# Shared k and q tiles behind the crossing of a two-way scan, and half matrices stored for its solve

## The chip, the cores and the metric

The kernel runs on one core of a Trainium2 chip. The metric is the device time of one execution in microseconds (us), the median of three runs. A core has five engines that run their own instruction streams beside each other: TensorE (PE in the profile: matmuls and transposes; its weight loads are PEld), VectorE (DVE), ScalarE (ACT), GpSimd (POOL) and SyncE (SP). SyncE issues all DMA transfers of this kernel, in order; 16 DMA engines carry them out.

## The reference

One layer of an encoder over 2048 positions of width 1024. A normalised input goes through one projection, whose columns feed two groups of heads. One group is windowed attention. The other, with four heads of 128, is a gated delta rule that is scanned forwards and backwards, with the outputs summed. Cut to the delta rule of one direction:

```python
decay = jnp.exp(jnp.where(incl, g[..., :, None] - g[..., None, :], -jnp.inf))
m = jnp.where(strict, jnp.einsum('bhncd,bhnsd->bhncs', k_beta, k) * decay, 0.0)
t_inv = triangular_solve(eye + m, eye)           # lower, unit diagonal
u = t_inv @ (v * beta)
w = t_inv @ (k_beta * exp(g))
a_intra = jnp.where(incl, jnp.einsum('bhncd,bhnsd->bhncs', q, k) * decay, 0.0)

def step(state, inp):
    v_new = u_i - w_i @ state
    o = (q_i * exp(g_i)) @ state + a_i @ v_new
    state = state * exp(g_last) + k_dec.T @ v_new
    return state, o

fwd = gated_delta_rule_chunked(q, k, v, g[:, :, 0], beta[:, :, 0])
bwd = flip(gated_delta_rule_chunked(flip(q), flip(k), flip(v), flip(g[:, :, 1]), flip(beta[:, :, 1])))
return fwd + bwd
```

The joined outputs of both groups go through an output projection and are added to the input.

## The kernel before

**Stages.** Phase A projects the input, convolves q, k and v, computes the attention and writes its results to DRAM. For each delta head h, `kq_d[h]` holds k and q there, 128 features by 2 by 2048 positions. Phase B does the delta heads one after the other. The 2048 positions are 16 chunks of 128, taken in four groups of four (c4).

- `pre_front(h)` loads k, q and v by groups, forms the products of k with k and with q for each chunk, and multiplies them by the decays into `ma` (L711). For each group and each direction d, a tile view `ma[d, c4]` holds, for 128 rows and four chunks, slot 0 (the matrix to be inverted) and slot 1 (the intra-chunk matrix). Slot 0 is stored to the DRAM buffer `m_d` at L716, one transfer for a group and direction: 128 rows by 4 chunks by 128 columns of float32.
- `solve(h)` reads only the four 32 by 32 diagonal blocks of each of these matrices back from `m_d`, as X (L739) and L (L740), in runs of 32 elements; inverts all of them at once on VectorE, a column after the other (L749, L753); and stores the inverses to `x_d` (L754).
- `invert(h)` loads these inverses as `xc` (L765), builds the full inverses from them with matmuls (L781), and writes them into slot 0 of `ma`.
- `scan(h)` runs 16 steps i. In each of them direction 0 takes chunk i and direction 1 chunk 15 - i. From step 1 on a step loads its chunk of k and q as `kqc` (L819), 128 KB, into one of four buffers of its direction, multiplies k by the state (`pk`, L821) and q by the state (`po`, L832), and updates the state (L839, L842). The two directions cross between steps 7 and 8: at step 8 direction 0 takes chunk 8, which direction 1 has taken at step 7.
- After step 12, and after the last, `post` normalises the finished groups of outputs. Between these, as work that fills TensorE, output products of the attention half run (`sw_units`, L596 to L598, with loads `mxs`, `xrs`, `zcs` and stores `part`). At the end `out_pair` does the output products of the delta half.

Front, solve and inversion of head h + 1 and the scan of head h overlap: two heads' `ma` tiles are held at a time, in two sets that alternate.

**Order.** The source order isn't the order on the engines. `set_order` builds a graph of all instructions with an estimated cost for each, plans the whole kernel in alternating passes from the front and from the back, keeps the best plan of the later passes, and pins the resulting order of each engine, SyncE's transfers included. A DMA counts there with 500 ns on SyncE, and with a share of a common bus that grows with its runs and their length.

**Lines touched.** L716 (the store of `m_d`), and in `scan` the load at L819 with its tile at L818 and its readers L821 and L832.

Of the kernel before, what the change touches and what calls it, by code (L numbers as in the profile page):

```python
# [7 lines left out]
F32 = mybir.dt.float32  # L8
# [7 lines left out]
P = 128  # L16
# [6 lines left out]
NQ = 8  # L23
EPS = 1e-6
NDEC = 1
LATE = ((0, 2), (1, 2), (1, 3), (0, 3), (2, 2), (3, 2), (3, 3), (2, 3), (4, 2), (5, 2), (6, 2), (7, 2), (7, 3), (6, 3), (5, 3), (4, 3))
WSB = 7
MXB = 8
# [518 lines left out]
def phase_b(ctx, wide, xe, ae, late, tc, t, ident, consts, hp, mix_dn, mix_sw, kq_d, v_d, zdn_d, zsw_d, dp, out):  # L547
    nc = tc.nc
    V, A, G, T = nc.vector, nc.scalar, nc.gpsimd, nc.tensor
    dma = nc.sync.dma_start  # L550
# [71 lines left out]
    halves = slice(0, 64), slice(64, P)  # L622
# [18 lines left out]
    def pre_front(h):  # L641
# [9 lines left out]
        ma = H["ma"] = {}  # L651
        m_d = dp.tile([2, NCH, 4 * (32 * P + 32)], F32, tag="m_d", name=f"m_d{h}", bufs=2)
        x_d = dp.tile([2, NCH, P, 32], F32, tag="x_d", name=f"x_d{h}", bufs=2)
        for n, c4 in enumerate(FRONT):
            s4 = slice(4 * c4, 4 * c4 + 4)
            cs = slice(c4 * 512, (c4 + 1) * 512)
            kq = q2[:, 2 * (n % 2) : 2 * (n % 2) + 2]
            dma(kq, kq_d[h][:, :, cs])
            vt = q2[:, 4 + n % 2]
            dma(vt, v_d[h][:, cs])  # L660
            gms = []
            for d in range(2):
                k = 2 * (n % 2) + d
                if k < 3:
                    gm = q3[:, k].rearrange("p (c i) -> p c i", c=4)
                else:
                    gm = q1.tile([P, 4, P], F32, tag="gm", name=f"dc{h}_{c4}_{d}", bufs=1)
                if h < NDEC:
                    dma(gm.rearrange("p c i -> p (c i)"), dec_d[h, d][c4])
                else:  # L670
                    src = gr_d[d].rearrange("(c h) i -> c h i", h=4)[s4, h]
                    dma(gm, src.partition_broadcast(P))
                    G.tensor_tensor(gm, gm, dmask[:, d : d + 1].to_broadcast([P, 4, P]), ALU.add)
                gms.append(gm)
                p = 3 - c4 if d else c4
                if p not in mp:
                    mp[p] = ma_tile(h, p)
                ma[d, c4] = mp[p][:, :, 1 - d :: 2]
            for j, ss in ((0, ssk), (1, ssq)):
                tr = ps_t.tile([P, 4, P], F32, tag="tr", name=f"tr{h}_{c4}_{j}")  # L680
                for c in range(4):
                    T.transpose(tr[:, c], kq[:, j, c * P : (c + 1) * P], ident)
                if j == 0:
                    ks[c4] = kv_tile("ks", h, n, f"ks{h}_{c4}")
                    A.activation(ks[c4], tr, AF.Copy)
                for c in range(4):
                    cc = 4 * c4 + c
                    src = ks[c4] if j == 0 else tr
                    jk = q1.tile([P, P], F32, tag="jk", name=f"jk{h}_{c4}_{j}_{c}", bufs=3)
                    A.activation(jk, src[:, c], AF.Square, accum_out=ss[:, cc : cc + 1])  # L690
            V.tensor_scalar(ssk[:, s4], ssk[:, s4], EPS, None, ALU.add)  # L691
            G.tensor_tensor(nk[:, s4], ssk[:, s4], pw[:, 0, :4], ALU.pow)  # L692
            V.reciprocal(ssk[:, s4], ssk[:, s4])
            V.tensor_tensor(
                bp[:, :, s4], beta[:, s4, h :: 4].rearrange("p c d -> p d c"),
                ssk[:, s4].unsqueeze(1).to_broadcast([P, 2, 4]), ALU.mult,
            )
            for c2 in range(2):
                gh = ps_g.tile([P, 2, 2, P], F32, tag="gh", name=f"gh{h}_{c4}_{c2}")
                for k in range(2):  # L700
                    c = 2 * c2 + k
                    T.matmul(
                        gh[:, k], kq[:, 0, c * P : (c + 1) * P], kq[:, :, c * P : (c + 1) * P], start=True, stop=True
                    )
                for k in range(2):
                    c = 2 * c2 + k
                    cc = 4 * c4 + c
                    for d in range(2):
                        if h >= NDEC:
                            A.activation(gms[d][:, c], gms[d][:, c], AF.Exp, bias=ngc[:, d, cc, h : h + 1])  # L710
                        V.scalar_tensor_tensor(  # L711
                            ma[d, c4][:, c], gh[:, k], bp[:, d, cc : cc + 1],
                            gms[d][:, c : c + 1].to_broadcast([P, 2, P]), ALU.mult, ALU.mult,
                        )
            for d in range(2):
                dma(m_d[d, s4, : P * P].rearrange("u (i j) -> i u j", j=P), ma[d, c4][:, :, 0])  # L716
            tr = ps_t.tile([P, 4, P], F32, tag="tr", name=f"trv{h}_{c4}")
            for c in range(4):
                T.transpose(tr[:, c], vt[:, c * P : (c + 1) * P], ident)
            vs[c4] = kv_tile("vs", h, n, f"vs{h}_{c4}")  # L720
            for c in range(4):
                cc = 4 * c4 + c
                A.activation(vs[c4][:, c], tr[:, c], AF.Copy, scale=nk[:, cc : cc + 1])
            if h:
                for k in range(FILLF[h - 1][n]):
                    fill(1, bank(k % 2))
# [80 lines left out]
    def scan(h, H):  # L807
        ks, vs, ck, ma = (H[k] for k in ("ks", "vs", "ck", "ma"))
        oacc = H["oacc"] = {}
        st = {}  # L810
        for i in range(NCH):
            for d in range(2):
                c = i if d == 0 else NCH - 1 - i
                c4, cl = c // 4, c % 4
                sc = slice(c * P, (c + 1) * P)
                nm = f"{h}_{d}_{i}"
                if i:
                    kqc = rp.tile([P, 2, P], F32, tag=f"kqc{d}", name=f"kqc{nm}", bufs=4)  # L818
                    dma(kqc, kq_d[h][:, :, sc])  # L819
                    pk = ps_s.tile([P, P], F32, tag="pk", name=f"pk{nm}")  # L820
                    T.matmul(pk, kqc[:, 0], st[d], start=True, stop=True)  # L821
                    r = rp.tile([P, P], F32, tag="r", name=f"r{nm}")
                    V.scalar_tensor_tensor(
                        r, pk, negc[:, d, c, h : h + 1], vs[c4][:, cl], ALU.mult, ALU.add
                    )
                else:
                    r = vs[c4][:, cl]
                py = ps_s.tile([P, P], F32, tag="py", name=f"py{nm}")
                po = ps_s.tile([P, 3, P], F32, tag="po", name=f"po{nm}", bufs=2)
                T.matmul(py, ma[d, c4][:, cl, 0], r, start=True, stop=True)  # L830
                if i:
                    T.matmul(po[:, 2], kqc[:, 1], st[d], start=True, stop=True)  # L832
                if i < NCH - 1:
                    yk = rp.tile([P, P], F32, tag="yk", name=f"yk{nm}", bufs=3)
                    A.activation(yk, py, AF.Copy, scale=ck[:, d, c : c + 1])  # L835
                y = rp.tile([P, P], F32, tag="y", name=f"y{nm}", bufs=3)
                A.activation(y, py, AF.Copy)
                if i < NCH - 1:
                    T.matmul(po[:, 0], ks[c4][:, cl], yk, start=True, stop=True)  # L839
                    s_new = rp.tile([P, P], F32, tag=f"S{d}", name=f"S{nm}", bufs=3)  # L840
                    if i:
                        V.scalar_tensor_tensor(  # L842
                            s_new, st[d], egt[:, d, c, h : h + 1], po[:, 0], ALU.mult, ALU.add
                        )
                    else:
                        V.tensor_copy(s_new, po[:, 0])
                    st[d] = s_new
                T.matmul(po[:, 1], ma[d, c4][:, cl, 1], y, start=True, stop=True)
                if c4 not in oacc:
                    oacc[c4] = rp.tile([P, 4, P], F32, tag="oacc", name=f"oacc{h}_{c4}", bufs=5)  # L850
                oa = oacc[c4][:, cl]
                if i == 0:
                    A.activation(oa, po[:, 1], AF.Copy)
                elif i < NCH // 2:
                    A.activation(oa, po[:, 2], AF.Copy, scale=egc[:, d, c, h : h + 1])
                    V.tensor_tensor(oa, po[:, 1], oa, ALU.add)
                else:
                    V.scalar_tensor_tensor(oa, po[:, 2], egc[:, d, c, h : h + 1], oa, ALU.mult, ALU.add)
                    V.tensor_tensor(oa, po[:, 1], oa, ALU.add)
            if i == 12:  # L860
                post(h, H, (1, 2))
        post(h, H, (0, 3))
# [48 lines left out]
    with tc.using_default_side("right"):  # L911
        rp = pool("rp", 2)
# [504 lines left out]
```

## Time and profile before

| | |
|---|---|
| time, median of 3 runs | 1269.36 us (1263.35 to 1274.25) |
| time of the profiled execution | 1270.01 us |
| its span, from the first to the last instruction | 1268.0 us |
| mean granted TensorE clock | 0.989 |
| DMA packets, bytes | 232294, 206.39 MB |
| HBM read, written | 139.84 MB, 65.08 MB |

The profile is one execution. Its page gives the busy time of each engine; the DMA queues; the chain of work that ended last, followed back from the last instruction; the costliest groups of instructions; and the DMA issues with the median time from issue to landing. L716 means line 716 of the kernel before. Further views of the same trace count the busy time of stretches of it, or list the instructions of one line or one engine in order of time. A releaser is the instruction whose end let a waiting one start. "DMA share" is the mean busy share of the 16 DMA engines.

### The profile page before, as it was taken

What the parts mean: (1) busy time and instruction counts of PE and PEld (TensorE: products, weight loads), DVE (VectorE), ACT (ScalarE), POOL (GpSimd) and SP (SyncE); (2) the same over time, 40 slices, a digit from 0 to 9 for tenths busy, and PEclk for the clock granted to TensorE, in tenths of its full rate; (3) what the DMA queues carried; (4) which work ended last, traced back from release to release, by engine and by line L of the source; (5) the groups of instructions that cost most, each with busy time, mean ns of one, the idle gap of its engine ahead of it and who ended that gap; (6) DMA issues with size and microseconds to landing.
All of it is one profiled execution on the core that took longest, in us unless ns stands there. A gap on an engine that the chain in (4) does not pass through costs nothing.

```text
span 1268.0 us, 22351 instructions
## 1 busy us (share of the span) xinstructions
PE 1210.5 (95%) x7018; PEld 1037.4 (82%) x7018; DVE 953.7 (75%) x2320; ACT 725.8 (57%) x2167; POOL 529.2 (42%) x845
## 2 busy tenths in 40 slices
PE   6999999999999999999999998999889899999898
PEld 5998888788889988887777777888789689888776
DVE  4523689999854379999995587698769779876765
ACT  6432476666534367766665438658557845685421
POOL 2243454763302276556422304613742441670541
PEclk9999999999999999999999999999889999999999
DMA  7553243513544434431016848967955875854785
GB/s 259 172 160 125 75 154 100 173 60 102 166 145 125 144 110 137 137 96 55 34 51 207 238 141 245 264 189 207 268 166 174 236 200 152 242 175 122 238 269 199
DMA packets 232294, 206.39 MB, mean 163 GB/s; under 512 B 49137, under 2 KB 181873, under 8 KB 232177
## 3 DMA queue, kind: packets, MB, share of 16 engines
q1 hardware_dynamic: 232176, 204.97, 53.0%
q8 instruction: 56, 0.92, 0.3%
q14 instruction: 62, 0.50, 0.1%
HBM read 139.84 MB, written 65.08 MB: 162 GB/s over the span
## 4 chain that ended last, share of the span: by engine, by line
PE 67%; DVE 13%; DMA 9%; ACT 4%; issue 3%; POOL 1%; SPq 1%; DVEq 0%; ACTq 0%; POOLq 0%
PE pf_c L199 5%; PE pf_c L201 5%; PE pf_c L200 5%; PE pf_z L199 4%; PE pf_z L200 4%; PE pf_z L201 4%; PE pi L781 3%; PE pq_q L212 2%; PE pq_q L211 2%; PE pt L390 2%; PE pq_q L210 2%; DMA xc<-x_d 2%; PE py L830 2%; PE po L839 2%; PE pcs L596 2%
## 5 line engine op out<-in xcount | busy, mean ns | idle before, releaser
L199 PE MATMUL pf_c<-xhi,wh_c 128*128 128x512 f32 x384 | 155.7, 405 | 0.8 <-DVE acc L269 0.8
L200 PE MATMUL pf_c<-xlo,wh_c 128*128 128x512 f32 x384 | 154.7, 403 | 0.0
L201 PE MATMUL pf_c<-xhi,wl_c 128*128 128x512 f32 x384 | 154.3, 402 | 0.0
L269 DVE SCALAR_TENSOR_TENSOR acc<-pf_c,cw,acc 128x512 f32<-128x512 f32 (+1 forms) x192 | 140.8, 742 | 2.6 <-POOL acc L259 0.7
L385 POOL TENSOR_SCALAR pr<-pr,st 128x384 f32<-128x384 f32 (+1 forms) x128 | 79.4, 639 | 98.0 <-DVE st L383 71.2
L394 ACT ACTIVATE ph<-pt 128x512 fp32r<-128x512 f32 x92 | 53.0, 595 | 60.5 <-PE pt L390 51.5
L376 ACT ACTIVATE pr<-pr,st 128x384 f32<-128x384 f32 (+1 forms) x128 | 76.2, 597 | 17.8 <-DVE st L372 17.4
L199 PEld LDWEIGHTS pf_c<-xhi,wh_c 128*128 128x128 f32 x384 | 72.5, 189 | 13.5 <-DVE acc L269 1.3
L201 PEld LDWEIGHTS pf_c<-xhi,wl_c 128*128 128x128 f32 x384 | 72.3, 188 | 12.9
L200 PEld LDWEIGHTS pf_c<-xlo,wh_c 128*128 128x128 f32 x384 | 72.4, 188 | 11.6
L835 ACT ACTIVATE yk<-py,ck 128x128 f32<-128x128 f32 x120 | 43.9, 366 | 62.0 <-PE py L830 61.2
L372 DVE CUSTOM_DVE_ANT_0 pr<-s,mask,sink 128x384 f32<-128x384 f32 (+1 forms) x128 | 73.4, 593 | 2.5 <-PE s L371 1.0
L211 PE MATMUL pq_q<-wh_q,xlo 128*128 128x256 f32 x256 | 72.1, 282 | 0.0
L212 PE MATMUL pq_q<-wl_q,xhi 128*128 128x256 f32 x256 | 71.9, 281 | 0.0
L210 PE MATMUL pq_q<-wh_q,xhi 128*128 128x256 f32 x256 | 71.4, 280 | 0.0
L390 PE MATMUL pt<-ident,pr 128*128 128x128 f32 x368 | 69.5, 274 | 1.8 <-DVE pl L395 1.1
L395 DVE TENSOR_TENSOR pl<-pt,ph 128x512 fp32r<-128x512 f32 x92 | 61.6, 681 | 6.1 <-ACT ph L394 5.6
L390 PEld LDWEIGHTS pt<-ident,pr 128*128 128x128 f32 x368 | 47.8, 140 | 20.4 <-DVE pl L395 4.4
L596 PE MATMUL pcs<-wohs,mhs 128*128 128x512 f32 x128 | 58.3, 456 | 4.4 <-ACT mhs L590 2.7
L692 POOL TENSOR_TENSOR nk<-ssk,pw 128x4 f32<-128x4 f32 x16 | 16.5, 1029 | 106.8 <-DVE ssk L691 106.6
L597 PE MATMUL pcs<-wohs,mls 128*128 128x512 f32 x128 | 56.1, 438 | 1.7 <-DVE mls L591 1.7
L598 PE MATMUL pcs<-wols,mhs 128*128 128x512 f32 x128 | 55.0, 429 | 0.0
(324 smaller groups left out, 4029.4 us busy)
## 6 DMA issues: line engine op xcount, KB each, us to landing
kqc<-kq_d SPq DMA_DIRECT2D x120, 128.0 KB, 3.1
ws_c<-wt SPq DMA_DIRECT2D x48, 256.0 KB, 3.5
xr<-x SPq DMA_DIRECT2D x16, 512.0 KB, 5.3
k_q<-kq_d SPq DMA_DIRECT2D x16, 512.0 KB, 5.6
mxs<-mix_sw SPq DMA_DIRECT2D x32, 256.0 KB, 3.7
xrs<-x SPq DMA_DIRECT2D x32, 256.0 KB, 3.7
part<-xrs SPq DMA_DIRECT2D x32, 256.0 KB, 2.6
xrd<-part SPq DMA_DIRECT2D x32, 256.0 KB, 4.1
```

The costliest lines, as they stand in the source:

```text
L199: T.matmul(ps, hi[:, k, cs], xhi[b][:, k], start=(k == 0), stop=False)
L200: T.matmul(ps, hi[:, k, cs], xlo[b][:, k], start=False, stop=False)
L201: T.matmul(ps, lo[:, k, cs], xhi[b][:, k], start=False, stop=(k == KC - 1))
L210: T.matmul(ps[:, :n], xh, hi[:, k, :n], start=(k == 0), stop=False)
L211: T.matmul(ps[:, :n], xl, hi[:, k, :n], start=False, stop=False)
L212: T.matmul(ps[:, :n], xh, lo[:, k, :n], start=False, stop=(k == KC - 1))
L269: V.scalar_tensor_tensor(av, ps[:, lo:], cw[:, i, k : k + 1], av, ALU.mult, ALU.add)
L372: V.tensor_tensor_reduce(pr[j][:, :n], ps[:, :n], mask[:, lo * P : hi * P], 1.0, sink[:, hh : hh + 1], ALU.add, ALU.min, accum_out=nm[:, j ...
L376: A.activation(pr[j][:, :n], pr[j][:, :n], AF.Exp, bias=nm[:, j : j + 1], scale=-1.0, accum_out=den[:, j : j + 1])
L385: G.tensor_scalar(pr[j][:, :n], pr[j][:, :n], den[:, j : j + 1], 1.0, ALU.mult, ALU.mult)
L390: T.transpose(pt[:, j], pr[j][:, (kb - lo) * P : (kb - lo + 1) * P], ident)
L596: T.matmul(ps, mh[:, k], wh[:, k], start=(k == 0), stop=False)
```

## The change

At steps 8, 9 and 10 of the scan neither direction loads k and q any more. Each takes the tile that the other direction loaded for the same chunk: at step 8 the one of step 7, at step 9 that of step 6, at step 10 that of step 5. Loads start again at step 11. The tiles still have four buffers for each direction, so that the load of step 11 takes the buffer of step 4, that of step 12 the buffer of step 5, and so on.

The store of `m_d` leaves out the two off-diagonal quarters of each matrix. The two diagonal quarters, 64 rows by 64 columns each, are stored by a transfer of their own. `solve` reads as before; the 32 by 32 blocks that it reads all lie in these quarters. `halves` is the pair of slices 0 to 64 and 64 to 128, which the kernel has already.

```diff
+HALF = 8
+KEEP = 3
...
             for d in range(2):
-                dma(m_d[d, s4, : P * P].rearrange("u (i j) -> i u j", j=P), ma[d, c4][:, :, 0])
+                for b in halves:
+                    dma(m_d[d, s4, : P * P].rearrange("u (i j) -> i u j", j=P)[b, :, b], ma[d, c4][b, :, 0, b])
...
         oacc = H["oacc"] = {}
-        st = {}
+        st, kqs = {}, {}
         for i in range(NCH):
...
                 if i:
-                    kqc = rp.tile([P, 2, P], F32, tag=f"kqc{d}", name=f"kqc{nm}", bufs=4)
-                    dma(kqc, kq_d[h][:, :, sc])
+                    if HALF <= i < HALF + KEEP:
+                        kqc = kqs[1 - d, c]
+                    else:
+                        kqc = kqs[d, c] = rp.tile([P, 2, P], F32, tag=f"kqc{d}", name=f"kqc{nm}", bufs=4)
+                        dma(kqc, kq_d[h][:, :, sc])
                     pk = ps_s.tile([P, P], F32, tag="pk", name=f"pk{nm}")
```

## The prediction

> **What bounds the kernel now.** The first thing read is the head of the page: the span and the busy time of each engine.
>
> ```profile
> span 1268.0 us, 22351 instructions
> ...
> PE 1210.5 (95%) x7018; PEld 1037.4 (82%) x7018; DVE 953.7 (75%) x2320; ACT 725.8 (57%) x2167; POOL 529.2 (42%) x845
> ```
>
> TensorE is busy for 1210.5 of 1268.0 us, so all that can be won without less matrix work lies in 57.5 us, and this change takes away no matmul. The question is where those 57.5 us are. The second view is the busy time by stretch: first the projections and attention (28 to 640 us), and the output product (1180 to 1268 us).
>
> ```profile
> core 0: us, PE busy (x) PEld busy (x) DVE busy (x) ACT busy (x) POOL busy (x), PEclk, DMA share, GB/s
> ...
> 28.00:640.00 612.00, 608.17 (x3407) 519.66 (x3408) 460.91 (x968) 343.75 (x810) 282.37 (x442) 1.00 0.38 120
> ...
> 1180.00:1268.00 88.00, 80.19 (x343) 63.02 (x343) 57.05 (x92) 25.77 (x71) 35.78 (x40) 1.00 0.72 233
> ```
>
> Neither stretch holds a line of the change. Between them I cut the delta part at the places where TensorE drops: three junctions, where one head's scan ends and the next head's inversion and the front of the head after that run (782 to 820, 866 to 926, 980 to 1030), and four stretches in the middle of the scans.
>
> ```profile
> 782.00:820.00 38.00, 32.73 (x217) 29.13 (x217) 28.93 (x75) 29.41 (x98) 26.72 (x56) 0.96 0.95 272
> 866.00:926.00 60.00, 52.10 (x330) 45.13 (x328) 47.88 (x151) 44.32 (x189) 33.90 (x55) 0.94 0.90 244
> 980.00:1030.00 50.00, 43.70 (x267) 36.87 (x267) 38.89 (x125) 35.22 (x149) 25.10 (x48) 0.97 0.85 230
> 940.00:980.00 40.00, 40.00 (x298) 37.40 (x296) 36.76 (x115) 27.22 (x107) 9.57 (x10) 1.00 0.54 167
> 1040.00:1080.00 40.00, 40.00 (x299) 37.50 (x298) 37.79 (x122) 22.09 (x69) 5.39 (x7) 1.00 0.53 160
> 820.00:860.00 40.00, 38.82 (x268) 35.32 (x267) 34.72 (x111) 20.98 (x74) 6.08 (x9) 1.00 0.60 185
> 1120.00:1160.00 40.00, 40.00 (x319) 38.48 (x319) 30.21 (x81) 28.67 (x92) 17.18 (x21) 1.00 0.53 154
> ```
>
> The columns are length, then busy time (and instructions) of PE, PEld, DVE, ACT and POOL, then granted clock, DMA share and GB/s. In the middle of a scan TensorE is full (40.00 of 40.00 three times) and the DMA engines are half idle (0.53 to 0.60). In the junctions it is the reverse: TensorE idles 5.3 + 7.9 + 6.3 = 19.5 us, the clock falls to 0.96, 0.94 and 0.97 (38 x 0.04 + 60 x 0.06 + 50 x 0.03 = 6.6 us more), and DMA stands at 0.95, 0.90 and 0.85. The pool that this change can touch is thus about 26 us, and it lies in the junctions. The chain of waits through the middle junction shows what it hangs on.
>
> ```profile
> 881.83 0.55 SPq L889
> 882.43 6.82 DMA x_d<-X
> 889.27 4.05 DMA xc<-x_d
> ...
> 904.27 4.15 DMA m_d<-ma
> ...
> 924.46 6.88 DMA xrs<-x
> ```
>
> Four landings, 6.82 + 4.05 + 4.15 + 6.88 = 21.9 of the 60 us, are DMA; SyncE's own queue has 0.55 us.
>
> **The change, part by part.** First the transfers concerned.
>
> ```profile
> kqc<-kq_d SPq DMA_DIRECT2D x120, 128.0 KB, 3.1
> ...
> m_d<-ma SPq DMA_DIRECT2D x20, 256.0 KB, 5.6
> ...
> m_d<-xhi_h SPq DMA_DIRECT2D x8, 256.0 KB, 6.1
> ...
> m_d<-xlo_h SPq DMA_DIRECT2D x4, 256.0 KB, 4.6
> ```
>
> Of the 120 kqc loads, 3 steps x 2 directions x 4 heads = 24 go. The 20 + 8 + 4 = 32 stores of 256 KB become 64 of 64 KB (64 rows x 4 chunks x 256 bytes). A 256 KB store moves 512 runs of 512 bytes; its pair moves 2 x 256 runs of 256 bytes: as many packets, half the bytes. What is a packet worth? Two stretches with nearly full DMA, one of large packets (884 to 890 us) and one of small (914 to 921 us):
>
> ```profile
> q1 hardware_dynamic: 1952, 1.80, 91.1%
> ```
>
> ```profile
> q1 hardware_dynamic: 4986, 1.33, 93.4%
> ```
>
> The first: 0.911 x 16 engines x 6 us / 1952 = 44.8 ns at 922 bytes; the second: 0.934 x 16 x 7 / 4986 = 21.0 ns at 267 bytes. The straight line between them is 0.0363 ns a byte, so 29.9 ns for 512 bytes and 20.6 ns for 256.
>
> *Loads shared.* 24 x 256 packets x 29.9 ns / 16 = 11.5 us of DMA time and, by the issue row below, 24 x 0.52 us of SyncE go. Where are steps 8 to 10? Counting the state products by stretch (two instructions to one product, two products to a step):
>
> ```profile
> 820.00:840.00 20.00, 1.94 (x11) 1.00 0.64 204
> 840.00:860.00 20.00, 3.46 (x18) 1.00 0.55 166
> ...
> 1060.00:1080.00 20.00, 3.47 (x18) 1.00 0.55 163
> ```
>
> 18 instructions are 9 products, 4.5 steps, so a step takes 4.4 us. The first head's steps 8 to 10 fall into 840 to 860 us, the others' by the same count into the other mid-scan stretches: where TensorE is full. The work that hides these loads is the scan's own matmuls and the filling output products; taking the loads away leaves TensorE as the bound. I take 0; the bound from the other side is the 1.2 us idle in 820 to 860. Were that cover gone, a load would cost its landing, 3.1 us.
>
> *Halved stores.* Here the place is the junction: the middle one holds all eight stores of its head, from the first to the last of SyncE's order:
>
> ```profile
> 866.90 0.38 SPq L716 DMA_DIRECT2D m_d<-ma  x1
> ...
> 910.02 0.63 SPq L716 DMA_DIRECT2D m_d<-ma  x1
> ```
>
> Per junction they save 8 x 512 x (29.9 - 20.6) ns / 16 = 2.4 us of DMA time. If all of it counted, 2.4 us; but only 21.9 of 60 us of the chain is DMA, so I take 2.4 x 0.365 = 0.9, three times 2.6 us. The first head's stores come before its load of X, beside projections that keep TensorE full (19.98 of 20 us), and count 0:
>
> ```profile
> 721.71 0.61 SPq L739 DMA_DIRECT2D X<-m_d  x1
> ```
>
> ```profile
> 700.00:720.00 20.00, 19.98 (x95) 16.26 (x94) 12.48 (x34) 8.76 (x35) 5.29 (x5) 1.00 0.91 266
> ```
>
> *More issues.* SyncE's cost of one:
>
> ```profile
> L819 SPq DMA_DIRECT2D kqc<-kq_d x120: 517/524/1625, 782.1 to 1159.8; - x120
> ```
>
> ```profile
> L716 SPq DMA_DIRECT2D m_d<-ma x20: 360/462/922, 691.2 to 1014.1; - x20
> ```
>
> Eight added stores a junction at 0.46 us with some 0.08 between them are 4.3 us of SyncE, ahead of xc loads, part stores and front loads queued behind them. If all of it delayed the chain: 4.3 us a junction, 13 in all; if none: 0. The chain gives SyncE 0.55 of 60 us, so I stand near the lower end, with one thing counted in full: the load of X waits for the second half of the last pair, one issue later: 0.54 x 3 = 1.6 us.
>
> *A shorter lead.* The shared tile is free only after the later direction has read it. With four buffers, loading step 12 waits for the other direction's step 10 where it waited for its own step 8. Its lead falls from about 3.5 to about 1.5 steps, 6.6 us at 4.4 us a step.
>
> ```profile
> DMA to landing us min/median/max: 2.4/3.1/7.0
> ```
>
> The row (kqc) says it fits at the median by 3.5 us: 0 taken; the other end is a rival below. The planner orders all engines anew from the changed list; the trace cannot show that order. It may win or lose something in the junctions; I bound this by half their pool, 13 us either way, and take 0.
>
> Sum: 0 - 2.6 + 1.6 + 0 = -1.0 us on the profiled execution's 1270.0 (1268.0 of span and 2.0 around it). The median of the runs, 1269.36, stands 0.6 lower, so about 1268. A measurement here tells about 1% from no change: the three runs lie between 1263.35 and 1274.25.
>
> **Rivals.** *The lead is too short (slower).* Place: step 12 of each scan, which in the first three heads runs into a junction. A load that lands in 7.0 us, issued behind a SyncE wait of the length that the kqc loads already have,
>
> ```profile
> SPq L819 <- PE po L839: 50.3, 32, 4.1
> ```
>
> arrives after 4.1 + 7.0 = 11.1 us against a lead of 6.6: 4.5 us late, both directions together, so 4 x 4.5 = 18 us: 1287. It decides from the point where wait and landing pass 6.6 us. Against it: the median landing, and that loads 13 to 15 keep longer leads. Chance 0.13.
>
> *Small writes are dearer (slower, or level).* No row shows a write of 256 bytes to HBM; the price of 20.6 ns rests on stretches dominated by small reads. If such a write costs twice that, 41.2 ns, a junction gains 8 x 512 x 11.3 / 16 = 2.9 us of DMA time instead of losing 2.4. In full on the chain, three times: +8.7; with half of the 13 us of added issues, +15: so 1278 to 1284. For it: DMA is nearly full there; against it: the chain's DMA share. Chance 0.10, half of it within 1%. The Trainium skill, "DMA: Bandwidth & Descriptors", section Specifications, gives 512 bytes as the least transfer at line rate and says that below it the engine does a read-modify-write; no run here shows that yet.
>
> *The junctions open (faster).* The landings of x_d and xc:
>
> ```profile
> DMA to landing us min/median/max: 3.1/6.4/6.8
> ```
>
> ```profile
> DMA to landing us min/median/max: 2.2/4.0/7.6
> ```
>
> If with 2.4 us less store traffic the new order lets x_d land in its least time, 6.4 - 3.1 = 3.3 us earlier, and xc 4.0 - 2.2 = 1.8 earlier, a junction shortens by 5.1 us, three by 15: 1254. For it: both are on the chain at DMA 0.90. Against it: 2.4 us of traffic in 60 is little, and the stores of these heads are only a few of the transfers that they queue among. Chance 0.17.
>
> *The change is hidden:* that is the forecast itself, 0.60.
>
> **How the numbers follow.** Time 1268, of the likeliest case. Faster by over 1% (below 1256.7): 0.17. Slower by over 1% (above 1282.1): 0.13 and half of 0.10, 0.18. Within: 0.60 + 0.05 = 0.65. The range runs from just under the open junctions' 1254 to just above the upper end of the dear writes, 1253 to 1284; the likeliest case alone, with the order's spread trimmed by what three junctions rarely do together, is 1259 to 1277. Left out are most of the short lead and a tail of the faster case, some 0.2.
>
> **What would show it.** kqc must be x96 and m_d x64 at 64 KB, with written bytes down by 4.2 MB, and the DMA share of the whole span, which is now
>
> ```profile
> q1 hardware_dynamic: 232176, 204.97, 53.0%
> ```
>
> falls to about 51% (11.5 us and 4 x 2.4 us of 1268). Right: TensorE's busy time as before, mid-scan stretches still full, junctions within 2 to 3 us of their old idle time. Wrong: the state product (L821 here) waiting for kqc at step 12 (short lead); 256-byte stretches at more than 30 ns a packet (dear writes); x_d and xc landing near 3 us with a granted clock of 1.00 in the junctions (open); or a large shift in junctions in which none of these transfers is late, which would be the new order alone.

## The result: 1.0% slower

| | before | after |
|---|---|---|
| median of 10 runs each | 1267.75 us (1262.70 to 1275.76) | 1280.59 us (1275.16 to 1285.74) |
| ratio, 95% interval | | 1.0101 [1.0078, 1.0125] |
| span of the profiled execution | 1268.0 us | 1283.9 us |
| HBM written | 65.08 MB | 60.88 MB |

The profiled execution of after is the slowest of its ten (1285.74 us), so its trace shows more loss than the median does. Line numbers in the views of a run are those of its own kernel. The head of the page of after and its DMA queue:

```profile
span 1283.9 us, 22364 instructions
...
PE 1212.4 (94%) x7018; PEld 1039.8 (81%) x7018; DVE 958.3 (75%) x2320; ACT 726.8 (57%) x2167; POOL 530.6 (41%) x845
...
q1 hardware_dynamic: 226160, 197.63, 51.5%
...
HBM read 136.69 MB, written 60.88 MB: 154 GB/s over the span
```

The traffic is what the change says: 4.2 MB less written, DMA share 51.5% for 53.0%. TensorE does the same work in nearly the same time, 1212.4 us for 1210.5. What has grown is its idle time, from 57.5 to 71.5 us. Where it lies shows in the busy time by stretch (columns as in the prediction), with two mid-scan stretches first, then the three junctions, each 60 us, and the step from the last scan to the output product; below it are the rows of before for the first and the third junction, in stretches of the same 60 us:

```profile
840.00:880.00 40.00, 40.00 (x288) 36.95 (x287) 38.95 (x129) 25.53 (x107) 7.50 (x10) 1.00 0.51 157
1060.00:1080.00 20.00, 20.00 (x152) 18.77 (x150) 18.23 (x58) 11.07 (x37) 4.03 (x6) 1.00 0.33 97
780.00:840.00 60.00, 52.00 (x315) 44.52 (x314) 39.35 (x116) 40.85 (x147) 32.20 (x66) 0.94 0.92 242
880.00:940.00 60.00, 49.23 (x329) 43.77 (x328) 45.41 (x129) 43.69 (x173) 38.20 (x70) 0.97 0.85 225
980.00:1040.00 60.00, 50.38 (x315) 41.87 (x313) 49.04 (x155) 41.18 (x174) 26.32 (x48) 1.00 0.84 225
1180.00:1200.00 20.00, 14.86 (x81) 11.97 (x82) 10.78 (x30) 10.74 (x45) 5.46 (x7) 0.88 0.69 214
```

```profile
780.00:820.00 40.00, 34.73 (x227) 30.60 (x227) 30.35 (x79) 31.39 (x106) 28.47 (x62) 0.96 0.95 272
820.00:840.00 20.00, 19.52 (x128) 17.31 (x127) 16.89 (x52) 9.63 (x30) 3.72 (x7) 1.00 0.64 204
...
980.00:1040.00 60.00, 52.03 (x308) 43.69 (x308) 44.81 (x143) 39.13 (x162) 31.37 (x65) 0.94 0.82 228
```

The two mid-scan stretches are full, as those of before were. The junctions idle 8.0 + 10.8 + 9.6 = 28.4 us, where before they idled 5.8 + 7.9 + 8.0 = 21.6 (the middle one by the row of 866 to 926 us in the prediction). So 6.8 of the 14.0 us of added idle time lie in the junctions; the last stretch idles 5.1 us for 4.0 in the 20 us at the same distance from the end of the scans before (1168 to 1188 us), and the rest is spread. The two transfers themselves, by tile, the stores first (the view lists the 64 under three names of their source):

```profile
L719 SPq DMA_DIRECT2D m_d<-ma x40: 574/608/1562, 698.9 to 1020.4; - x40
L719 SPq DMA_DIRECT2D m_d<-xhi_h x16: 575/616/1122, 773.8 to 1024.4; - x16
L719 SPq DMA_DIRECT2D m_d<-xlo_h x8: 607/615/995, 798.9 to 1009.3; - x8
```

A store of a quarter of the bytes does not cost SyncE less than the full one did (360/462/922 ns in the first of its rows) but more: 608 ns at the median, 574 at the least. By these medians a pair costs 1.22 us where one store cost 0.46. The loads:

```profile
L825 SPq DMA_DIRECT2D kqc<-kq_d x96: 517/556/1130, 790.4 to 1172.9; - x96
its engine sat idle before it (us, times) until:
  DVE S L848: 6.3, 7
  DVE r L829: 1.6, 3
  DVE oacc L865: 1.0, 2
  DVE S L852: 0.2, 1
```

Before the matmuls that read k and q, TensorE waits for VectorE alone; a load is in none of the rows. The stores' first start, 698.9 us for 691.2, says that part of the difference arises ahead of every changed instruction.

### The profile page after: what moved, and what is told of

The parts are those of the page before. It is cut to its first block, busy times and chain, and to the rows that moved or that the text cites. A ratio compares the mean times of both kernels' runs of the same rounds, so it can differ in the third digit from the quotient of the medians.

```text
span 1283.9 us, 22364 instructions
## 1 busy us (share of the span) xinstructions
PE 1212.4 (94%) x7018; PEld 1039.8 (81%) x7018; DVE 958.3 (75%) x2320; ACT 726.8 (57%) x2167; POOL 530.6 (41%) x845
## 3 DMA queue, kind: packets, MB, share of 16 engines
q1 hardware_dynamic: 226160, 197.63, 51.5%
HBM read 136.69 MB, written 60.88 MB: 154 GB/s over the span
## 4 chain that ended last, share of the span: by engine, by line
PE 62%; DVE 16%; DMA 10%; ACT 4%; issue 4%; POOL 2%; SPq 1%; DVEq 0%; ACTq 0%; POOLq 0%
PE pf_c L203 4%; PE pf_c L202 4%; PE pf_c L201 4%; PE pf_z L203 4%; PE pf_z L201 4%; PE pf_z L202 4%; PE pi L784 4%; DVE acc L271 3%; PE pt L392 2%; PE pq_q L214 2%; PE pq_q L213 2%; PE pq_q L212 2%; PE py L836 2%; PE pcs L599 2%; PE pcs L598 2%
## 5 line engine op out<-in xcount | busy, mean ns | idle before, releaser
L203 PEld LDWEIGHTS pf_c<-xhi,wl_c 128*128 128x128 f32 x384 | 72.7, 189 | 12.8
L201 PEld LDWEIGHTS pf_c<-xhi,wh_c 128*128 128x128 f32 x384 | 72.7, 189 | 11.6
L193 DVE TENSOR_TENSOR wl_c<-ws_c,wh_c 128x512 fp32r<-128x512 f32 x48 | 39.7, 828 | 20.1 <-ACT wh_c L192 14.9
```

The costliest lines, as they stand in the source:

```text
L201: T.matmul(ps, hi[:, k, cs], xhi[b][:, k], start=(k == 0), stop=False)
L203: T.matmul(ps, lo[:, k, cs], xhi[b][:, k], start=False, stop=(k == KC - 1))
```

## The experiments

Three theories were open: **A**, that the loss is the new order that the planner made; **B**, that an edit costs (short lead, dear small writes, issues); later **C**, that of these it is the added issues. To part them, most kernels below keep the old order, that of the kernel before: the program plans the kernel before, and pins every engine of the changed kernel to that order. Loads that the change removes are left out of it, and the stores that replace one stand in its place. Each kernel was timed in five rounds beside the kernel before on its chip; ratios are to that.

### The order held, and the order alone

`both_oldorder` is the whole change in the old order. `null_2401`, `null_2405` and `null_2399` are the kernel before with no instruction changed, planned with another latency for a DMA:

```diff
-LAG = {"PE": 205, "DVE": 140, "Activation": 160, "Pool": 120, "SP": 2400}
+LAG = {"PE": 205, "DVE": 140, "Activation": 160, "Pool": 120, "SP": 2401}
```

> Both edits as in the change, but every engine keeps the order that the planner gave the kernel before: only the 24 loads are missing and each store is two. Theory A (the loss of 1.0% is the new order alone; the edits themselves cost nothing or win 1 to 3 us): 1264 to 1269 us, ratio to before 0.996 to 1.002. Theory B (the edits cost: a short lead at step 12, dearer small writes, more issues on SyncE): the loss stays without the new order, 1277 to 1283 us, ratio 1.007 or more. B's short lead should be at its worst here, since the order was not made for it.

> The kernel before with not one instruction or transfer changed; the planner alone counts a DMA's latency as 2401 ns where it counted 2400, which gives another order. Theory A: slower than before like the change, 1272 to 1285 us, ratio 1.003 to 1.014. Theory B: within 0.3% of before, since no transfer differs.

> The kernel before, unchanged in every instruction, planned with a DMA latency of 2405 ns instead of 2400: another order again. If the order that the kernel before has is one of the better of those that the planner finds: slower by 0.3 to 1.3%, 1270 to 1283 us. If the loss with 2401 was an accident: as often faster as slower, 1260 to 1272 us.

> As the run before with 2399 ns. Same two expectations: 1270 to 1283 us, or as often faster as slower, 1260 to 1272 us.

| kernel | median us | ratio | 95% interval |
|---|---|---|---|
| both_oldorder | 1277.58 | 1.0083 | 1.0058 to 1.0109 |
| null_2401 | 1276.56 | 1.0081 | 1.0050 to 1.0113 |
| null_2405 | 1275.37 | 1.0076 | 1.0048 to 1.0103 |
| null_2399 | 1272.17 | 1.0040 | 1.0014 to 1.0066 |

Both theories met half of what they expected. One nanosecond in the planner's table makes the kernel 0.4 to 0.8% slower: of the four orders tried for the same instructions, the kernel before has the best. But the change loses 0.8% also where the order is held, so A alone is not the explanation; whether its own order adds anything can't be told, as the difference between 1.0101 and 1.0083 is within the intervals. For the rest of the study it follows that an edit can be priced only in a held order.

### Each part by itself, planned anew

`halves_own` has `KEEP = 0`, `keep_own` the full stores.

> The halved stores alone, all k and q loads kept, planned anew. Theory A: some order of its own, anywhere from 1266 to 1285 us, and not additive with the other part (the two parts' losses need not sum to 12.8 us). Theory B with dear small writes or issues: about 1280 us; with the short lead: about 1268 us.

> The shared tiles alone, full stores, planned anew. Theory A: anywhere from 1266 to 1285 us, not additive with the other part. Theory B with the short lead: about 1280 us; with dear small writes: about 1268 us.

Measured: halved stores 1269.16 us, 1.0032 [1.0008, 1.0056]; shared tiles 1271.57 us, 1.0051 [1.0024, 1.0078]. Each has drawn an order of its own, and the nulls show that a draw alone moves as much. Neither reading of B is told apart by these two.

### Each part in the old order

`halves_oldorder` and `keep_oldorder` are the parts; `keep2_oldorder` shares for two steps (`KEEP = 2`); `rowsplit_oldorder` splits the stores but keeps their bytes:

```diff
-dma(m_d[d, s4, : P * P].rearrange("u (i j) -> i u j", j=P), ma[d, c4][:, :, 0])
+for b in halves:
+    dma(m_d[d, s4, : P * P].rearrange("u (i j) -> i u j", j=P)[b], ma[d, c4][b, :, 0])
```

> The halved stores alone, every engine in the order of the kernel before. Both edits in that order lost 0.8% (about 10 us); this run and the next divide it. Theory C (the issues: 64 stores at 0.61 us of SyncE in place of 32 at 0.46, 0.75 us more a pair, 6 us more a head in the junction): most of the loss is here, 1272 to 1279 us, ratio 1.004 to 1.010. Theory L (the short lead of step 12): 1263 to 1268 us, ratio within 0.3% of before.

> The shared tiles alone, full stores, in the order of the kernel before. Theory C: 1263 to 1268 us. Theory L: most of the loss is here, 1272 to 1279 us, with SyncE held at the load of step 12 by the other direction's state product.

> Shared tiles for two steps (8 and 9) instead of three, full stores, in the order of the kernel before: 16 loads fewer instead of 24, and no load waits for a buffer that was released less than about three steps before. Theory L: the loss of the kernel with three shared steps in this order goes, 1263 to 1268 us. If the loss comes from the missing loads themselves (the later transfers of SyncE move forward), about two thirds of it stays.

> Each full store as two, of 64 rows with all 128 columns: the number of stores of the change, but the bytes and 512-byte runs of the kernel before; all loads kept; in the order of the kernel before. Theory C: as the halved stores in this order, or up to 3 us slower for the bytes. A theory in which the 256-byte runs cost: as the kernel before, 1263 to 1268 us.

| kernel | median us | ratio | 95% interval |
|---|---|---|---|
| halves_oldorder | 1271.86 | 1.0045 | 1.0019 to 1.0071 |
| keep_oldorder | 1268.27 | 1.0014 | 0.9987 to 1.0042 |
| keep2_oldorder | 1270.16 | 1.0039 | 1.0014 to 1.0063 |
| rowsplit_oldorder | 1275.24 | 1.0077 | 1.0050 to 1.0105 |

The halved stores lose, at the lower edge of what C expected (1272 to 1279 us); the shared tiles can't be told from the kernel before; and the row split, which changes nothing but the number of stores, loses 0.77%, about 9.8 us. Theory L, the short lead, falls: three shared steps lose little or nothing, and two, which don't have the short lead, are not better. What two shared steps lose isn't explained by these runs. The row split's stores, by tile:

```profile
L723 SPq DMA_DIRECT2D m_d<-ma x40: 575/608/1148, 691.0 to 1021.8; - x40
```

The same 608 ns as in after, with twice the bytes: between these two the issue time goes with the rows of the store, not with its bytes. Neither traffic nor a later landing carries the loss of the row split: its DMA share is 52.8% for 53.0% before, and its stores take 4.9 us from issue to landing at the median for 5.6 before.

### More issues, fewer bytes

`quadsplit_oldorder` stores each matrix in four, of 32 rows (`for b in quads`, with all columns). `halved_one_oldorder` stores half the bytes in one issue, columns 0 to 63 of all rows. It leaves out half of what the solve needs and packs the rest to 64 columns a row, from which X and L are read in runs of 32 as before, so it inverts other blocks than it should, and its output is not the reference's:

```diff
-dma(m_d[d, s4, : P * P].rearrange("u (i j) -> i u j", j=P), ma[d, c4][:, :, 0])
+dma(m_d[d, s4].rearrange("u (i j) -> i u j", j=64), ma[d, c4][:, :, 0, :64])
```

> Each full store as four, of 32 rows with all 128 columns; loads and bytes as before; in the order of the kernel before. Doubles the suspected cost: 96 added issues where two per store added 32 and lost 0.77%. Theory C (the number of issues on SyncE costs, about 9 us for 32): 1290 to 1300 us, ratio 1.018 to 1.026. If the loss of the row split was only a disturbed order (a lottery that any touch draws from): 1270 to 1280, ratio 1.003 to 1.010, no more than for two.

> 32 stores as before, one issue each, but only columns 0 to 63 of all rows: as many bytes and 256-byte runs as the change, without its added issues; in the order of the kernel before. The solve reads blocks of the same size and number from the packed buffer, so it inverts other blocks than it should, and the output is not the reference's. Theory C: the bytes alone win, 1260 to 1265 us, ratio 0.995 to 1.000. If 256-byte writes are dear: slower than before, 1269 to 1275 us.

Measured: four stores 1291.45 us, 1.0207 [1.0176, 1.0238]; half the bytes in one 1260.20 us, 0.9956 [0.9936, 0.9976]. Both are as C had it. 32 added issues cost about 9.8 us and 96 about 26, or 0.31 and 0.27 us an issue. The bytes win 0.44%, about 5.6 us, in a kernel whose X and L loads also read a denser buffer (X lands in 5.4 us at the median for 6.1 before), so this is the most that the bytes alone can be given. In that kernel the last X load starts at 1014.6 us, where before it was 1021.23 (the last value of its row):

```profile
L723 SPq DMA_DIRECT2D m_d<-ma x20: 360/442/998, 692.1 to 1007.2; - x20
...
L748 SPq DMA_DIRECT2D X<-m_d x4: 539/542/746, 721.8 to 1014.6; - x4
```

With the same bytes as before in two stores, and in four, the last X load starts 7.1 and 20.4 us later than before, so the loss is there ahead of the last solve (row split first, then the X loads and the stores of the split in four):

```profile
L746 SPq DMA_DIRECT2D X<-m_d x4: 592/604/667, 723.4 to 1028.3; - x4
```

```profile
L746 SPq DMA_DIRECT2D X<-m_d x4: 606/606/611, 729.6 to 1041.7; - x4
...
L723 SPq DMA_DIRECT2D m_d<-ma x80: 303/443/1338, 691.9 to 1035.1; - x80
```

Gain and cost add up: -0.44 + 0.77 = +0.33%, and the halved stores measured +0.45 [0.19, 0.71].

### Where an issue costs

`quadsplit_h0` splits in four the stores of the first head alone (`for b in quads if h == 0`). `xcmerge3` loads the solved blocks in pairs, into three buffers of twice the size:

```diff
-xc = qb.tile([P, 4, 32], F32, tag="xc", name=f"xc{h}_{d}_{c4}", bufs=4)
-dma(xc, x_d[d, 4 * c4 : 4 * c4 + 4].rearrange("u i c -> i u c"))
+if hi % 2 == 0:
+    xp[d] = qb.tile([P, 8, 32], F32, tag="xc", name=f"xc{h}_{d}_{hi}", bufs=3)
+    dma(xp[d], x_d[d, u0 : u0 + 8].rearrange("u i c -> i u c"))
```

> Stores in four as before, but those of the first head alone (8 stores become 32), which are issued beside the last projections, ahead of the first junction; everything else and the order as in the kernel before. Theory C with its place (an issue costs only in a junction, where SyncE and DMA are both nearly full and TensorE waits on what lies behind): 1263 to 1268 us, ratio within 0.25% of before. If an added issue costs the same wherever it stands: a quarter of the 2.07% of all heads, 1274 to 1278 us, ratio about 1.005.

> The other sign and another transfer: the kernel before, in its order, with its 32 loads of inverted blocks (xc, 64 KB) merged in pairs to 16 of 128 KB, each in the place of the earlier one of its pair; three buffers. Bytes and runs as before, 16 issues fewer, all in the junctions. Theory C (0.2 to 0.3 us an issue): 3 to 5 us faster, 1261 to 1264 us, ratio 0.996 to 0.998. If it was the splitting of the stores that cost (the wait for a pair's later half) and not the slots of SyncE: no gain, 1265 to 1270 us.

Measured: 1275.56 us, 1.0069 [1.0049, 1.0089], and 1274.76 us, 1.0056 [1.0036, 1.0075]. Both miss what C with its place expected. The first comes out as its other reading had it, by which an added issue costs the same wherever it stands (1274 to 1278 us); the second meets neither of its two. So the first head's stores do cost. The traces say how. The kernel before, the store of the first solve and the state product by line and tile:

```profile
L754 SPq DMA_DIRECT2D x_d<-X x4: 325/520/583, 768.1 to 1076.9; - x4
```

```profile
L821 PE MATMUL pk<-S,kqc x240: 270/275/581, 800.6 to 1177.0; 128*128 128x128 f32 x120
```

The kernel with the first head's stores in four: stores and X load by tile, then the same two rows.

```profile
L723 SPq DMA_DIRECT2D m_d<-ma x44: 302/452/815, 695.4 to 1020.4; - x44
...
L746 SPq DMA_DIRECT2D X<-m_d x4: 607/607/611, 733.2 to 1027.7; - x4
```

```profile
L761 SPq DMA_DIRECT2D x_d<-X x4: 326/520/612, 779.7 to 1079.1; - x4
```

```profile
L831 PE MATMUL pk<-S,kqc x240: 270/275/377, 812.4 to 1180.3; 128*128 128x128 f32 x120
```

From the first store to the first X load it was 721.7 - 691.2 = 30.5 us and is 733.2 - 695.4 = 37.8: 7.3 us more (the first store itself starts 4.2 later, for no reason in the stores). The kernel with all stores in four agrees, with 37.7 us; in kernels of the old order whose stores are not split it takes 29.8 to 31.8. In this time the stores hold SyncE for about 19 us, where they held it for 3.8. They do not land later: SyncE's wait at the load of L for a store's landing falls from 3.7 to 1.8 us. The delay goes on: the solve ends 11.6 us later (779.7 for 768.1), the first scan starts 11.8 later (812.4 for 800.6), 7.6 of it behind the first store. At the start of the last state product 3.3 are left of it; what made good the rest these traces don't show, and the execution as a whole is 5.8 us longer.

Nor does TensorE stay full beside these stores. Its busy time from 690 to 735 us, before and with the first head's stores in four, and what ScalarE waits in this stretch for `zs`, weights of the projections that still run there:

```profile
690.00:735.00 45.00, 43.25 (x206) 35.09 (x205) 23.77 (x61) 24.44 (x98) 11.95 (x11) 1.00 0.89 243
...
690.00:735.00 45.00, 39.33 (x190) 31.82 (x188) 22.06 (x60) 19.96 (x80) 9.93 (x9) 1.00 0.71 203
```

```profile
ACT zhi L240 <- DMA zs<-wt: 13.7, 9, 4.5
...
ACT zhi L245 <- DMA zs<-wt: 19.9, 7, 9.3
```

TensorE is busy for 3.9 us less (some of it because the whole execution runs 4.2 us later); with all stores in four it is 37.2 of 45, and in kernels of the old order whose stores are not split 41.2 to 43.3. The loads of `zs` stand in the same queue of SyncE as the stores. So two things hang on this queue here: the X load with the solve and the scan behind it, and the projections whose full TensorE was to hide the stores.

The merged loads show another thing. What SyncE waits for at the merged load, by the view of waits (us in total, times, longest us; the lines named are readers of the loaded tile):

```profile
SPq L777 <- POOL iv L793: 5.3, 2, 5.1
...
SPq L777 <- POOL xlo_h L810: 3.7, 1, 3.7
...
SPq L777 <- DVE iv L793: 3.1, 1, 3.1
```

The fourth load of a head stands at the head of SyncE's queue until a buffer of its first is free, and all of the queue stands behind it. These waits come to 12 us; before, no wait of SyncE at this load (L765) was longer than 1.4 us. What the 16 saved issues are worth can't be seen beside them, so the run tells nothing for or against C.

### The same stores from another queue

Here the stores of the halved-stores kernel, or of the kernel before, are issued from ScalarE, at the place of its old order where the plan had them start. `act_second`: the second of each pair; `act_both`: all 64; `act_full`: the 32 full stores.

```diff
-dma(m_d[d, s4, : P * P]...
+q = nc.scalar.dma_start if b.start else dma
+q(m_d[d, s4, : P * P]...
```

> The halved stores alone in the order of the kernel before, but the second store of each pair is issued from ScalarE, at the point of its order where the plan had the store begin; SyncE has 32 stores as before, each of half the rows. Theory C (a slot of SyncE costs, since all of its queue stands behind it): the loss of the halved stores goes and the bytes' gain appears, 1259 to 1267 us, ratio 0.994 to 1.001. If the splitting itself costs (X waits for the later of two), or ScalarE's queue is held by the store: 1269 to 1276 us.

> The kernel before and its order, its 32 full stores issued from ScalarE and none from SyncE. Theory C: 32 slots fewer on SyncE at some 0.24 to 0.29 us of gain each: 4 to 9 us faster, ratio 0.993 to 0.997. If ScalarE's order is held by the stores as long as SyncE's was: no gain or a loss, ratio 1.000 to 1.010.

> The halved stores alone in the order of the kernel before, all 64 issued from ScalarE, none from SyncE. Theory C: bytes and slots both gain, 1255 to 1263 us, ratio 0.990 to 0.998. If ScalarE is held by them: 1269 to 1280 us.

Measured: 1272.13 us, 1.0036 [1.0013, 1.0059]; 1271.73 us, 1.0038 [1.0023, 1.0053]; 1282.44 us, 1.0127 [1.0102, 1.0153]. None wins, and all three miss what C expected of them. ScalarE's issue times, by tile, the full stores and then all halves:

```profile
L725 ACTq DMA_DIRECT2D m_d<-ma x20: 366/392/463, 691.9 to 1016.8; - x20
```

```profile
L725 ACTq DMA_DIRECT2D m_d<-ma x40: 581/597/1034, 691.7 to 1028.3; - x40
```

An issue holds ScalarE about as long as SyncE, 366 ns at the least for 128 rows and 581 for 64. So C in its narrow form, that a slot of SyncE costs, does not hold: 32 fewer of them won nothing. A wider form, by which the issue costs on whichever of these two queues it stands, fits the three runs; they don't show it, as each store also got a new place among ScalarE's own work. No kernel of the study that computes the reference was faster than the kernel before.

## Why the prediction was wrong

The forecast was 1268 us, which is no change; the kernel takes 1280.59 us, and its loss is clear of the interval. That the time lies in the range (1253 to 1284) is owed to the allowance for dear small writes, which the runs do not bear out. Step by step:

- **What bounds the kernel**: right in the main. TensorE is full in the mid-scan stretches shown of both traces, and the junctions hold 6.8 of the 14.0 us of idle time that the change added. The rest came elsewhere.
- **Loads shared, 0**: not contradicted. In the held order it is +0.14% [-0.13, +0.42].
- **Halved stores, -2.6 us**: right in sign. Half the bytes in one issue gave -0.44% [-0.64, -0.24], about -5.6 us, between the -2.6 taken and the bound of three times 2.4.
- **More issues, +1.6 us**: this is the step that failed, as the size of a term. 32 added stores measured +0.77% [+0.50, +1.05], about +9.8 us, close to the upper bound of 13 that was worked out and set aside. Three things in it were wrong. An added store was given the 0.46 us of a full one; it takes 0.61, and the store that it splits takes 0.61 too, so a pair adds 0.76 us of SyncE. SyncE's small piece in the chain (0.55 of 60 us) was taken as its weight; the measured price of 0.27 to 0.31 us for an added issue shows that it isn't (a transfer that is issued later lands later, and the chain may book that as DMA; this was not followed). And the first head's stores were given 0 because TensorE was full beside them; the run with its stores alone in four lost 0.69%, for they stand ahead of the load that starts the solve and among the loads on which the full TensorE itself hangs.
- **A shorter lead, 0, with a rival at +18 us**: the 0 was right. No read of `kqc` waits for a load in after, and in the old order three shared steps, with the short lead, were no worse than two without it.
- **The new order, 0 within 13 us**: the bound was right in size: three other orders of the same instructions cost 0.40 to 0.81%, 5 to 10 us. Most of the loss of this change is there in the old order too.
- **Rival of dear small writes**: not borne out. With the issues unchanged, writes in runs of 256 bytes made the kernel faster. The Trainium skill, "DMA: Bandwidth & Descriptors", section Specifications, speaks of a read-modify-write below 512 bytes; no run here shows a price of it. The Trainium skill, "DMA: Bandwidth & Descriptors", section "Rules for kernel authors", advises one transfer of 128 partitions over two of disjoint halves. Here that holds, at +0.77%; the page gives shared DMA engines as the reason, where these traces show 0.61 us of issue time for each half.
- **Rival of the open junctions**: half the bytes in one issue did make the kernel 5.6 us faster, a third of the 15 us, but not by the landings that the rival named: in that trace x_d lands in 6.4 us at the median as before, and xc in 3.6 for 4.0. In the change the added issues outweigh this gain.

What stays open: the median change is +12.8 us where -1.0 was forecast. The cost given to the issues was 8.2 us too small and the gain given to the bytes 3.0 us too small, which leaves 8.6 us that no single run accounts for. In the old order the parts sum to +0.45 + 0.14 = 0.59%, the whole is 0.83 [0.58, 1.09], and planned anew it is 1.01 [0.78, 1.25]. The intervals allow the two parts to be all; they also allow a little of the two together, and of the new order. That the price of a store is the time of its issue, and not something else that comes with one more store, is argued from the traces: no run changed the one without the other.

## What to carry to other kernels

Splitting a transfer to save bytes pays the issue time a second time, on a queue in which every later transfer stands behind it. Weigh the saved DMA time against the measured issue time of the new shape. Count the issues on the way to the load that starts the next stage, even where the matrix engine is full beside them: its own loads may stand in the same queue. A queue's small share in the chain of waits was no measure here of what a delay in it costs. Where a planner orders the whole program, hold its order when you price an edit, and plan the unchanged program again with a trifle moved to see how much a draw of the order is worth.

## What the runs showed of the hardware that was not expected

The time that an engine is held by issuing a store doesn't follow its size. At the least, 128 rows of four 512-byte runs took 360 ns on SyncE and 366 on ScalarE; 64 rows took 574 to 582, alike with runs of 256 and of 512 bytes and on both engines; 32 rows took 302. Medians in SyncE's queue, each for the largest group of its stores, were 462, 608 and 443 ns. The shape is not all: the four full stores that the view of before lists under `xlo_h` took 582 to 782 ns on SyncE, and on ScalarE 367 to 399. Why the 64-row form is the dearest the traces don't show.
